# Probabilities by values in a chunk-attention trunk: three float32r products of split operands in place of one float32 product

## The chip, the cores and the metric

One core of one Trainium2 chip runs the whole program in one launch; the other seven cores are idle. The metric is the device time of one execution in microseconds (us). The kernel before was run three times: median 928.1 us, from 927.41 to 928.38.

Two number formats matter. A float32 matmul is carried out by TensorE in two passes, and the profile shows two records for each such instruction. A float32r matmul is one pass over operands that were rounded to fewer mantissa bits when they were written. To get float32 accuracy from float32r, an operand is split: the high part is the value rounded to float32r, the low part is the value minus the high part, again rounded. The product is then high by high plus low by high plus high by low, three passes into the same accumulator.

## The reference

Two layers. Each multiplies the 256 rows of `x` by one wide input projection and cuts the result into the inputs of three groups: chunk attention (8 heads of 128), gated linear attention (GLA, 4 heads), and cross-attention into 256 memory rows (4 heads). Each group output is gated, and one output projection and a LayerNorm follow. Cut to the two groups that the change touches:

```python
def chunk_band_attention(q, k, v, rel_table):
    ...
    scores = jnp.einsum('bnqhd,bnkhd->bnhqk', qc, k_band) * (Dh ** -0.5)
    scores = jnp.where(valid, scores + bias, NEG_INF)
    p = jax.nn.softmax(scores, axis=-1)
    out = jnp.einsum('bnhqk,bnkhd->bnqhd', p, v_band)      # the product that changes

def gla_chunk_recurrence(q, k, v, log_g):                  # reads the GLA values v
    ...
    attn = jnp.einsum('bihd,bjhd,bijhd->bhij', qc, kc, decay)
    o_intra = jnp.einsum('bhij,bjhv->bihv', attn, vc)
    o_inter = jnp.einsum('bihd,bhdv->bihv', qc * jnp.exp(b), state)
    new_state = jnp.exp(b_last)[..., None] * state + jnp.einsum('bjhd,bjhv->bhdv', k_dec, vc)
```

## The kernel before

The program is a stream of weight pieces. Each piece is loaded by SyncE into `raw`, rounded by ScalarE into a high part `wh` (line 116), and VectorE subtracts to get the low part `wl` (line 117, both in `parts`). `raw`, `wh` and `wl` have four buffers each, so at most four pieces stand ready ahead of TensorE. TensorE multiplies each piece by the split activations and accumulates in `acc`, of which there are two. A piece of a 512-wide group is 16 matmuls; a piece of a values group (`w388`, 388 columns) is 12.

TensorE and SyncE run in the order in which the source issues instructions. VectorE and ScalarE run in an order that a scheduler fixed when the program was built. All four work strictly in that order.

The small work of the heads is written as Python generators. After every weight piece the source calls `tick()`, which counts one and lets at most one due generator issue its next step; the number that a generator yields is how many pieces must pass before its next step. At most two generators are active at a time. So head work is slipped in between pieces, and the pieces cover the time that VectorE and ScalarE need between a generator's steps. `finish(gens)` is the other way to drive them: it calls `tick()` until they are done, with no piece in between.

The order in a layer: memory keys and values; queries and keys of GLA (`G_BQK`); `values(0)` and `values(1)`; then the GLA generator is queued; `values(2)`, the queries and keys of heads 0 to 3, and their four `a_head` generators; `values(3)`, and the same for heads 4 to 7; and so on.

`values(i)` computes 388 of the 1552 columns of `asv`: columns 0 to 15 are the low-rank gate input, 16 to 527 the GLA values, 528 to 1551 the values of the eight attention heads. One ScalarE copy (line 792) moves each group from `acc` to `asv`, in float32.

The GLA generator `gla` has this chain, with the yields between its steps in brackets: transpose the gate input (line 339) [2]; gate products, then the cumulative decay `b_` (line 359), the decayed keys `kd` (line 366) and queries `qe` [6]; transpose `kd` (line 392) and copy it (line 394) [2]; `decayed` for the first two of six levels, the state products with the GLA values (line 404), the diagonal products, the states `st` (lines 414 and 417), the diagonal pairs (line 332) [5]; then three rounds, each with the products of two levels, the masked copies of their results (`keep`, line 334) and `decayed` for the next two levels [6]; [3]; and last the products of `pairs` and of `st` with the values and with `qe` (lines 448 and 458). `decayed` is VectorE (line 379), ScalarE twice (lines 381 and 382), VectorE twice (lines 384 and 385), each waiting for the one before.

`a_head` has four steps in one chain: scores and softmax [3], three transposes of the probabilities (line 523) and a ScalarE copy of them into one float32 tile `pT` (line 525) [2], the two float32 products with the values (lines 529 and 530), and a copy out. The first product has 256 moving columns, the second 128, since rows of the first 128 keys serve all 256 queries and those of the second 128 keys serve only the last 128.

Of the kernel before, what the change touches and what calls it, by code (L numbers as in the profile page):

```python
# [8 lines left out]
F32 = mybir.dt.float32  # L9
F32R = mybir.dt.float32r  # L10
# [3 lines left out]
ALU = mybir.AluOpType  # L14
# [4 lines left out]
P = 128  # L19
# [17 lines left out]
def hybrid_trunk_kernel(  # L37
# [7 lines left out]
    pe, dve, act, pool, sp = nc.tensor, nc.vector, nc.scalar, nc.gpsimd, nc.sync  # L45
# [6 lines left out]
    def tick():  # L52

        now[0] += 1
        while True:
            while waiting and len(active) < 2:
                active.append((waiting.pop(0), 0))
            due = [e for e in active if e[1] <= now[0]]
            if not due:
                return  # L60
            active.remove(due[0])
            g = due[0][0]
            after = next(g, None)
# [13 lines left out]
    per = enter("per")  # L77
# [10 lines left out]
    def nm(s):  # L88
        uid[0] += 1
        return f"{s}_{uid[0]}"  # L90

    def mm(o, l, r, start, stop):
        pe.matmul(o, l, r, start=start, stop=stop, skip_group_check=True)  # L93
# [4 lines left out]
    def scratch(shape, dtype=F32):  # L98
        return sc.tile(shape, dtype, name=nm("sc"), tag="sc")
# [14 lines left out]
    def parts(hi, lo, src):  # L114

        act.copy(hi, src)  # L116
        dve.tensor_tensor(lo, src, hi.bitcast(F32), op=ALU.subtract)  # L117
# [189 lines left out]
        pool.dma_start(ng, norm_g[l])  # L307
        return gw, gb, ng

    def gla(gw, gb, ng, gq, gk, lr, asv, yraw):  # L310
        gqf = gq.rearrange("p b t -> p (b t)")
        gkf = gk.rearrange("p b t -> p (b t)")
        pairs = [hd.tile([P, 4, CH], F32, name=nm("pairs"), tag=f"pairs{par}") for par in range(2)]
# [23 lines left out]
        pt = bank()  # L337
# [5 lines left out]
        pl = bank()  # L343
# [45 lines left out]
        pt = bank()  # L389
# [8 lines left out]
        for c in range(3):  # L398
            rs = slice((c % 2) * 64, (c % 2) * 64 + 64)
            t = c // 2  # L400
            for b in range(2):
                for par in range(2):
                    h = 2 * b + par
                    mm(kv[c % 2][par * 64:par * 64 + 64, (t * 2 + b) * P:(t * 2 + b + 1) * P],
                       kdT[rs, t * 2 + b, par * 64:par * 64 + 64],
                       asv[rs, t, 16 + h * P:16 + (h + 1) * P], True, True)
        diagonal = [bank()[:, :256], kv[1][:, 256:]]
        products(gkf, gqf, diagonal)
        st = hd.tile([P, 3, 2, P], F32, name=nm("st"), tag="st")
        for c in range(3):  # L410
            t = c // 2
            src = kv[c % 2].rearrange("p (g c) -> p g c", c=P)[:, t * 2:t * 2 + 2]
# [26 lines left out]
        po = [bank() for _ in range(2)]  # L439
        far = [bank() for _ in range(2)]  # L440
        at = [slice(i * CH, (i + 1) * CH) for i in range(2)]
        for t in range(2):
            for b in range(2):
                g = t * 2 + b
                for half in range(2):
                    for par in range(2):
                        h = 2 * b + par
                        mm(po[half][at[par], g * P:(g + 1) * P], pairs[par][at[half], g],
                           asv[at[half], t, 16 + h * P:16 + (h + 1) * P], g == 0, False)
        for odd, even in ((1, 2), (3, None)):  # L450
            for b in range(2):
                for c in (odd, even):
                    if c is not None:
                        for par in range(2):
                            g = (c // 2) * 2 + b
                            half = c % 2
# [3 lines left out]
        for par in range(2):  # L460
            for half in range(2):
                act.copy(on[par][at[half]], po[half][at[par]].rearrange("p (g c) -> p g c", c=P))
            half = 1 - par
# [33 lines left out]

    SCALE = P ** -0.5

    def a_head(h, load_bias, bias, q, k, asv, y):  # L500

        if h + 2 < 8:
            load_bias(h + 2)
        pb = bank()
        mm(pb[:, 0:128], q[:, 0:128], k[:, 0:128], True, True)
        mm(pb[:, 128:384], q[:, 128:256], k, True, True)
        s = scratch([P, 384])
        dve.scalar_tensor_tensor(s, pb[:, :384], SCALE, bias[h], op0=ALU.mult, op1=ALU.add)  # L508
        mx = small([P, 2], "mx", 4)
        zs = small([P, 2], "zs", 4)  # L510
        own = (slice(0, 128), slice(128, 384))
        for t in range(2):
            dve.tensor_reduce(mx[:, t:t + 1], s[:, own[t]], AX.X, ALU.max, negate=True)  # L513
        for t in range(2):
            act.activation(s[:, own[t]], s[:, own[t]], AF.Exp, bias=mx[:, t:t + 1], accum_out=zs[:, t:t + 1])  # L515
        dve.reciprocal(zs, zs)
        for t in range(2):
            dve.tensor_scalar(s[:, own[t]], s[:, own[t]], zs[:, t:t + 1], None, op0=ALU.mult)
        yield 3

        pt = bank()
        for i in range(3):
            pe.transpose(pt[:, i * P:(i + 1) * P], s[:, i * P:(i + 1) * P], ident)  # L523
        pT = scratch([P, 384])
        act.copy(pT, pt[:, :384])
        yield 2
        po = bank()
        v0 = 528 + h * P
        mm(po[:, 0:256], asv[:, 0, v0:v0 + P], pT[:, 0:256], True, False)
        mm(po[:, 128:256], asv[:, 1, v0:v0 + P], pT[:, 256:384], False, True)  # L530
        act.copy(y, po[:, :256])
        yield 2

# [219 lines left out]
    for l in range(L):  # L753
# [20 lines left out]
        gq = hd.tile([P, 2, T], F32, name=nm("gq"), tag="gq")  # L774
        gk = hd.tile([P, 2, T], F32, name=nm("gk"), tag="gk")
# [4 lines left out]
        gp = gla_inputs(l)  # L780
# [4 lines left out]
            dve.tensor_copy(lmask, lm)  # L785
            dve.tensor_tensor(eye, ident[:, :CH], ident[:, CH:], op=ALU.add)

        asv = per.tile([P, 2, 1552], F32, name=nm("asv"), tag="asv")

        def values(i):  # L790
            acc = as_group(w388[l, i], xq, 388)
            act.copy(asv[:, :, i * 388:(i + 1) * 388], acc[:, :, :388])

        def heads(g):
            t = hd.tile([P, 4, T], F32, name=nm("qk"), tag="qk", bufs=4)
# [5 lines left out]

        lr = hd.tile([P, 2, 48], F32R, name=nm("lr"), tag="qe")
        values(0)
        for i in (0, 32):
            act.copy(lr[:, :, i:i + 16], asv[:, :, :16])
        dve.tensor_tensor(lr[:, :, 16:32], asv[:, :, :16], lr[:, :, :16].bitcast(F32), op=ALU.subtract)
        values(1)
        if l == 0:
            sp.dma_start(res, xn.rearrange("(t p) d -> p t d", p=P))
        bias = {}  # L810
# [7 lines left out]
        if l > 0:  # L818
            finish(gens)
        yraw = [per.tile([P, 4, T], F32, name=nm("yr"), tag=f"yr{i}") for i in range(4)]  # L820
        gens = [[gla(*gp, gq, gk, lr, asv, yraw[0])]]
        waiting.extend(gens[0])
        for half in range(2):
            values(2 + half)
            q = heads(G_AQ0 if half == 0 else G_AQ1)
            k = heads(G_AK0 if half == 0 else G_AK1)
            gens.append([a_head(half * 4 + h, load_bias, bias, q[:, h], k[:, h], asv, yraw[1 + half][:, h]) for h in range(4)])
            waiting.extend(gens[-1])
        q = [hd.tile([P, 4, T], F32R, name=nm("mq"), tag="qk", bufs=4) for _ in range(2)]
        for i, a, b in ws_group(w512[l, G_MQ], xq):  # L830
# [7 lines left out]
        acc = as_group([[w512[l, G_BZ, h * 4 + pc // 2][:, pc % 2 * 512:pc % 2 * 512 + 512] for h in range(2)]  # L838
                        for pc in range(8)], xq, 512)
# [5 lines left out]
        for i, g in ((1, G_AZ0), (2, G_AZ1), (3, G_MZ)):  # L845
            y = operand()
# [150 lines left out]
```

## Time and profile before

| | before |
|---|---|
| median of three runs | 928.1 us |
| the profiled execution, its own time | 928.0 us |
| its span, first to last instruction | 926.2 us |
| TensorE busy | 918.4 us, 99% |
| VectorE busy | 586.0 us, 63% |
| ScalarE busy | 500.4 us, 54% |
| mean granted TensorE clock | 0.998 |

The span is 1.8 us shorter than the time of its execution, which also holds what lies ahead of the first and behind the last instruction. Busy time is a union: overlapping instructions of an engine count once. The ends of matmuls are modelled, and a matmul is still counted busy while the next one streams, so costs on TensorE are best read from start to start. In the rows of the timeline the columns are the start, the time from the first start to the last end of the merged instructions, the engine, the line, the operation, what is written and read, the shape of the stationary and of the moving operand, how many instructions were merged, and in brackets the engine's idle time before and what ended it. A float32 matmul counts as two.

### The profile page before, as it was taken

The numbers are of one execution on the slowest core, as the hardware profiler recorded it, in microseconds if no ns is written. First come the engines' busy times: TensorE is split into PE (matmuls) and PEld (weight loads), VectorE is DVE, ScalarE is ACT, GpSimd is POOL, SyncE is SP. The second block draws the span as 40 slices with busy tenths as digits, with TensorE's granted clock in tenths as the row PEclk, the third lists the DMA queues.
The fourth block names the chain that finished last, engine by engine and source line by source line (L and its number), as shares of the span: only waits on it lengthen the run. The fifth ranks groups of instructions, "written<-read, shape, count | busy, mean of one in ns | idle before, by whom it ended". The sixth has DMA issues, their size and how long they took to land.

```text
span 926.2 us, 14232 instructions
## 1 busy us (share of the span) xinstructions
PE 918.4 (99%) x5500; PEld 806.7 (87%) x5500; DVE 586.0 (63%) x808; ACT 500.4 (54%) x718; POOL 20.4 (2%) x44
## 2 busy tenths in 40 slices
PE   9999999999999999999999999999999999999997
PEld 7889998998888888888888899889888888888885
DVE  6764587656564666555577674966655555766665
ACT  6644485375454675433476445744844555754350
POOL 1000000000000000000000000000000000110000
PEclk9999999999999999999999999999999999999999
DMA  9956865645554566666665466565465545676652
GB/s 310 331 187 174 303 205 161 178 157 197 184 160 160 172 202 203 217 196 192 226 209 203 147 206 193 182 187 183 154 203 171 164 154 160 193 232 215 198 163 92
DMA packets 71253, 178.85 MB, mean 193 GB/s; under 512 B 7304, under 2 KB 31240, under 8 KB 70928
## 3 DMA queue, kind: packets, MB, share of 16 engines
q1 hardware_dynamic: 69120, 173.30, 57.9%
q0 software_dynamic: 1920, 4.36, 1.9%
q8 instruction: 43, 0.70, 0.3%
q10 hardware_dynamic: 144, 0.26, 0.1%
q14 instruction: 26, 0.21, 0.1%
HBM read 175.77 MB, written 2.10 MB: 192 GB/s over the span
## 4 chain that ended last, share of the span: by engine, by line
PE 98%; ACT 0%; DMA 0%; DVE 0%; SPq 0%; issue 0%; ACTq 0%
PE acc L93 89%; PE bk L93 8%; PE bk L523 1%; DMA raw<-w 0%; PE bk L558 0%; PE bk L587 0%; PE bk L491 0%; ACT wh L116 0%; ACT res L636 0%; DVE wl L117 0%; PE bk L392 0%; SPq L177 0%; ACT res L739 0%; PE bk L339 0%; DVE stats L724 0%
## 5 line engine op out<-in xcount | busy, mean ns | idle before, releaser
L117 DVE TENSOR_TENSOR wl<-raw,wh 128x1024 fp32r<-128x1024 f32 (+3 forms) x321 | 370.0, 1155 | 255.3 <-ACT wh L116 250.8
L116 ACT CAST wh<-raw 128x1024 fp32r<-128x1024 f32 (+3 forms) x321 | 318.0, 994 | 332.1 <-PE acc L93 237.5
L93 PE MATMUL acc<-x,wh 128*128 128x512 f32 x1248 | 398.1, 400 | 0.6 <-ACT wh L116 0.6
L93 PE MATMUL acc<-wh,x 128*128 128x512 f32 (+2 forms) x1236 | 357.3, 370 | 0.2
L93 PEld LDWEIGHTS acc<-x,wl 128*128 128x128 f32 x1248 | 234.3, 188 | 55.9 <-DVE wl L117 0.7
L93 PEld LDWEIGHTS acc<-wh,x 128*128 128x128 f32 x1236 | 227.0, 188 | 28.3 <-ACT wh L116 0.7
L93 PE MATMUL acc<-x,wl 128*128 128x256 f32 x1248 | 246.2, 279 | 0.3 <-DVE wl L117 0.3
L93 PE MATMUL acc<-wl,x 128*128 128x512 f32 (+2 forms) x618 | 227.9, 369 | 0.0
L93 PEld LDWEIGHTS acc<-x,wh 128*128 128x128 f32 x1248 | 192.0, 189 | 2.4 <-ACT wh L116 0.8
L93 PEld LDWEIGHTS acc<-wl,x 128*128 128x128 f32 x618 | 116.0, 188 | 14.6 <-DVE wl L117 0.4
L515 ACT ACTIVATE sc<-sc,mx 128x128 f32<-128x128 f32 (+1 forms) x32 | 14.4, 450 | 21.3 <-DVE mx L513 21.3
L508 DVE SCALAR_TENSOR_TENSOR sc<-bk,bias 128x384 f32<-128x384 f32 x16 | 8.9, 556 | 14.6 <-PE bk L93 14.6
L381 ACT ACTIVATE sc<-sc 128x512 f32<-128x512 f32 x12 | 7.6, 633 | 13.2 <-DVE sc L379 13.2
L117 DVE TENSOR_TENSOR x<-sc,x 128x512 fp32r<-128x512 f32 x20 | 13.3, 685 | 0.7 <-ACT x L116 0.7
L620 DVE SCALAR_TENSOR_TENSOR res<-res,acc 128x512 f32<-128x512 f32 x15 | 9.7, 684 | 6.1 <-PE acc L93 6.1
L116 ACT CAST x<-raw 128x1024 fp32r<-128x1024 f32 x5 | 5.3, 1051 | 14.5 <-DMA raw<-memT 12.0
L93 PE MATMUL bk<-qk,qk 128*128 128x128 f32 (+1 forms) x64 | 13.1, 326 | 0.0
L93 PE MATMUL bk<-sc,asv 128*128 128x256 f32 (+1 forms) x64 | 13.0, 326 | 0.0
L262 DVE SCALAR_TENSOR_TENSOR sc<-acc,sc 128x512 f32<-128x512 f32 x19 | 13.0, 682 | 0.0
L117 DVE TENSOR_TENSOR x<-res,x 128x512 fp32r<-128x512 f32 (+2 forms) x14 | 10.5, 765 | 3.6 <-ACT x L116 3.6
L117 DVE TENSOR_TENSOR x<-raw,x 128x1024 fp32r<-128x1024 f32 x5 | 6.1, 1225 | 10.3 <-ACT x L116 10.3
L116 ACT CAST x<-sc 128x512 fp32r<-128x512 f32 x20 | 11.8, 614 | 1.0 <-DVE sc L595 1.0
(205 smaller groups left out, 567.3 us busy)
## 6 DMA issues: line engine op xcount, KB each, us to landing
raw<-w SPq DMA_DIRECT2D x214, 512.0 KB, 4.0
raw<-w SPq DMA_DIRECT2D x64, 388.0 KB, 3.1
raw<-w SPq DMA_DIRECT2D x83, 256.0 KB, 3.3
bias<-relw SPq DMA_DIRECT2D x16, 192.0 KB, 3.6
res<-xT SPq DMA_DIRECT2D x4, 512.0 KB, 5.0
res<-xn SPq DMA_DIRECT2D x1, 2048.0 KB, 8.0
raw<-memT SPq DMA_DIRECT2D x4, 512.0 KB, 4.4
res<-memT SPq DMA_DIRECT2D x6, 256.0 KB, 6.1
```

The lines of the kernel that those rows point to most:

```text
L93: pe.matmul(o, l, r, start=start, stop=stop, skip_group_check=True)
L116: act.copy(hi, src)
L117: dve.tensor_tensor(lo, src, hi.bitcast(F32), op=ALU.subtract)
L262: dve.scalar_tensor_tensor(dst, a, scale, dst, op0=ALU.mult, op1=ALU.add)
L381: act.activation(dd, dd, AF.Abs)
L508: dve.scalar_tensor_tensor(s, pb[:, :384], SCALE, bias[h], op0=ALU.mult, op1=ALU.add)
L515: act.activation(s[:, own[t]], s[:, own[t]], AF.Exp, bias=mx[:, t:t + 1], accum_out=zs[:, t:t + 1])
L523: pe.transpose(pt[:, i * P:(i + 1) * P], s[:, i * P:(i + 1) * P], ident)
L620: dve.scalar_tensor_tensor(r, r, ALPHA, acc, op0=ALU.mult, op1=ALU.add)
```

## The change

The value columns of the eight attention heads are no longer kept in float32. `asv` is split in three: `gv` holds the first 528 columns in float32 (gate input and GLA values); `avh` (named `asv` in rows) holds the high parts of all 1024 attention value columns; `avl` holds the low parts, in two tiles of 512 columns. `values(i)` now makes one float32 copy or one `parts` pair (ScalarE cast, VectorE subtract) for each stretch of columns between the cuts 528 and 1040.

The second `avl` tile has the tag of `gv`: it takes the same memory. So it can be created only behind the last instruction that reads `gv`, which is the last value product of the GLA generator. `values(2)`, which fills columns 776 to 1163, needs that tile. So behind the eight pieces of `values(2)` stands a loop that calls `tick()` until `gla` has passed that point (`done_with`).

In `a_head` the ScalarE copy of the transposed probabilities becomes a `parts` pair, and the two float32 products become six float32r products.

```diff
-    def gla(gw, gb, ng, gq, gk, lr, asv, yraw):
+    def gla(gw, gb, ng, gq, gk, lr, gv, yraw, done_with):
...
                         mm(po[half][at[par], g * P:(g + 1) * P], pairs[par][at[half], g],
-                           asv[at[half], t, 16 + h * P:16 + (h + 1) * P], g == 0, False)
+                           gv[at[half], t, 16 + h * P:16 + (h + 1) * P], g == 0, False)
+        done_with.append(gv)
...
-    def a_head(h, load_bias, bias, q, k, asv, y):
+    def a_head(h, load_bias, bias, q, k, v, y):
...
-        pT = scratch([P, 384])
-        act.copy(pT, pt[:, :384])
+        ph, pl = scratch([P, 384], F32R), scratch([P, 384], F32R)
+        parts(ph, pl, pt[:, :384])
         yield 2
         po = bank()
-        v0 = 528 + h * P
-        mm(po[:, 0:256], asv[:, 0, v0:v0 + P], pT[:, 0:256], True, False)
-        mm(po[:, 128:256], asv[:, 1, v0:v0 + P], pT[:, 256:384], False, True)
+        (vh, vl), last = v, (1, 2)
+        for t, cs, ks in ((0, slice(0, 256), slice(0, 256)), (1, slice(128, 256), slice(256, 384))):
+            for i, (a, b) in enumerate(((vh, ph), (vl, ph), (vh, pl))):
+                mm(po[:, cs], a[:, t], b[:, ks], t == i == 0, (t, i) == last)
...
-        asv = per.tile([P, 2, 1552], F32, name=nm("asv"), tag="asv")
+        gv = per.tile([P, 2, 528], F32, name=nm("gv"), tag="gv")
+        avh = per.tile([P, 2, 1024], F32R, name=nm("asv"), tag="asv")
+        avl = [per.tile([P, 2, 512], F32R, name=nm("avl"), tag="avl")]
+        done_with = []
 
         def values(i):
             acc = as_group(w388[l, i], xq, 388)
-            act.copy(asv[:, :, i * 388:(i + 1) * 388], acc[:, :, :388])
+            if i == 2:
+                while not done_with:
+                    tick()
+                avl.append(per.tile([P, 2, 512], F32R, name=nm("avl"), tag="gv"))
+            c0, c1 = i * 388, (i + 1) * 388
+            cuts = [c0] + [c for c in (528, 1040) if c0 < c < c1] + [c1]
+            for a, b in zip(cuts, cuts[1:]):
+                src = acc[:, :, a - c0:b - c0]
+                if b <= 528:
+                    act.copy(gv[:, :, a:b], src)
+                else:
+                    half, at = divmod(a - 528, 512)
+                    parts(avh[:, :, a - 528:b - 528], avl[half][:, :, at:at + b - a], src)
...
-        gens = [[gla(*gp, gq, gk, lr, asv, yraw[0])]]
+        gens = [[gla(*gp, gq, gk, lr, gv, yraw[0], done_with)]]
...
+            gens.append([a_head(half * 4 + h, load_bias, bias, q[:, h], k[:, h],
+                                [x[:, :, h * P:(h + 1) * P] for x in (avh[:, :, half * 512:], avl[half])],
+                                yraw[1 + half][:, h]) for h in range(4)])
```

The order of TensorE's instructions, first layer, from the transposes of `kd` on. Before, weight pieces (rows that write `acc`) stand between the steps of GLA; `bk` is a bank of small results, `sc` a scratch tile.

```order
L93 MATMUL acc_1211<-x_273,wl_1214 128x256 x2
L392 MATMUL bk_1234<-ident,sc_1109 128x128 x4
L93 MATMUL acc_1211<-x_366,wh_1242 128x512 x2
...
L93 MATMUL bk_1302<-gq_525,gk_526 64x64
L93 MATMUL acc_1211<-x_509,wh_1341 128x512 x2
...
L93 MATMUL acc_1364<-x_509,wl_1433 128x256 x2
L93 MATMUL bk_1453<-sc_1290,sc_1289 64x64
...
L93 MATMUL bk_1454<-sc_1298,sc_1297 64x64
L93 MATMUL acc_1510<-x_273,wh_1512 128x512 x2
```

With the change:

```order
L93 MATMUL acc_1035<-wl_1197,x_509 128x388
L392 MATMUL bk_1213<-ident,sc_1113 128x128 x4
L93 MATMUL bk_1236<-gv_725,sc_1218 64x128 x4
...
L93 MATMUL bk_1237<-gq_525,gk_526 64x64
L93 MATMUL bk_1275<-sc_1225,sc_1224 64x64
...
L93 MATMUL bk_1329<-sc_1318,sc_1317 64x64
...
L93 MATMUL bk_1383<-sc_1380,sc_1379 64x64
...
L93 MATMUL bk_1423<-gv_725,pairs_1054 64x128
...
L93 MATMUL bk_1424<-st_1267,qe_1121 64x128
L93 MATMUL acc_1475<-x_273,wh_1477 128x512 x2
```

All steps of GLA from the transposes of `kd` to the last product of `st` and `qe` now stand in one block behind the last piece of `values(2)`, with no weight piece among them. The second layer has the same block.

VectorE, first layer, from the decayed keys `kd` (line 366) on. Before:

```order
L366 TENSOR_TENSOR sc_1109<-gk_526,sc_1109 128x512
L117 TENSOR_TENSOR wl_1265<-raw_1263,wh_1264 128x1024
L117 TENSOR_TENSOR wl_1342<-raw_1340,wh_1341 128x1024
L379 TENSOR_TENSOR sc_1285<-b_1104 128x512
L117 TENSOR_TENSOR wl_1367<-raw_1365,wh_1366 128x1024
L384 TENSOR_TENSOR sc_1289<-gk_526,sc_1285 128x512
L385 TENSOR_TENSOR sc_1290<-gq_525,sc_1285 128x512
L379 TENSOR_TENSOR sc_1293<-b_1104 128x512
L117 TENSOR_TENSOR wl_1389<-raw_1387,wh_1388 128x1024
L384 TENSOR_TENSOR sc_1297<-gk_526,sc_1293 128x512
```

With the change, the same stretch and, behind the mark, the last level:

```order
L366 TENSOR_TENSOR sc_1113<-gk_526,sc_1113 128x512
L117 TENSOR_TENSOR wl_1533<-raw_1531,wh_1532 128x1024
L379 TENSOR_TENSOR sc_1220<-b_1108 128x512
L117 TENSOR_TENSOR wl_1555<-raw_1553,wh_1554 128x1024
L117 TENSOR_TENSOR avl_727<-acc_1035,asv_726 128x2x264
L384 TENSOR_TENSOR sc_1224<-gk_526,sc_1220 128x512
L385 TENSOR_TENSOR sc_1225<-gq_525,sc_1220 128x512
L379 TENSOR_TENSOR sc_1228<-b_1108 128x512
...
L384 TENSOR_TENSOR sc_1379<-gk_526,sc_1375 128x512
L385 TENSOR_TENSOR sc_1380<-gq_525,sc_1375 128x512
L334 COPY_PREDICATED pairs_1054<-lmask,bk_1383 128x256
```

Behind the fourth weight piece (`wl_1555`) and the first `avl` rows VectorE does nothing but GLA until the last masked copy; its next weight piece stands behind the normalisation of the GLA output. ScalarE has the same gap. In `a_head` one VectorE subtraction of 128x384 is added behind ScalarE's cast of the transposed probabilities, once for each of 16 heads.

More of the change, by code (lines that the diff above doesn't have):

```diff
@@ L405, in gla @@
                        kdT[rs, t * 2 + b, par * 64:par * 64 + 64],
-                       asv[rs, t, 16 + h * P:16 + (h + 1) * P], True, True)
+                       gv[rs, t, 16 + h * P:16 + (h + 1) * P], True, True)
         diagonal = [bank()[:, :256], kv[1][:, 256:]]
@@ L804, in hybrid_trunk_kernel @@
         for i in (0, 32):
-            act.copy(lr[:, :, i:i + 16], asv[:, :, :16])
-        dve.tensor_tensor(lr[:, :, 16:32], asv[:, :, :16], lr[:, :, :16].bitcast(F32), op=ALU.subtract)
+            act.copy(lr[:, :, i:i + 16], gv[:, :, :16])
+        dve.tensor_tensor(lr[:, :, 16:32], gv[:, :, :16], lr[:, :, :16].bitcast(F32), op=ALU.subtract)
         values(1)
@@ L826, in hybrid_trunk_kernel @@
             k = heads(G_AK0 if half == 0 else G_AK1)
-            gens.append([a_head(half * 4 + h, load_bias, bias, q[:, h], k[:, h], asv, yraw[1 + half][:, h]) for h in range(4)])
+            gens.append([a_head(half * 4 + h, load_bias, bias, q[:, h], k[:, h],
+                                [x[:, :, h * P:(h + 1) * P] for x in (avh[:, :, half * 512:], avl[half])],
+                                yraw[1 + half][:, h]) for h in range(4)])
             waiting.extend(gens[-1])
```

## The prediction

> **What bounds the kernel now.** I read the page's busy shares first, then its chain of the work that ended last, then the stretch of the first layer in which GLA runs.
>
> ```profile
> PE 918.4 (99%) x5500; PEld 806.7 (87%) x5500; DVE 586.0 (63%) x808; ACT 500.4 (54%) x718; POOL 20.4 (2%) x44
> PE acc L93 89%; PE bk L93 8%; PE bk L523 1%; DMA raw<-w 0%; PE bk L558 0%; PE bk L587 0%; PE bk L491 0%; ACT wh L116 0%; ACT res L636 0%; DVE wl L117 0%; PE bk L392 0%; SPq L177 0%; ACT res L739 0%; PE bk L339 0%; DVE stats L724 0%
> ```
>
> TensorE is never without work, and the chain is TensorE's own line of matmuls: 89% weight pieces, 8% small products. So a nanosecond added to TensorE's work or to its waiting is a nanosecond of the time, and work on VectorE or ScalarE costs nothing as long as TensorE doesn't come to wait for it. The view by stretches shows the 26 us behind the last piece of `values(2)` in the first layer (start:end, length, then busy time and instructions of TensorE, its weight loads, VectorE, ScalarE and GpSimd; granted clock, share of the DMA engines, GB/s):
>
> ```profile
> 124.33:150.66 26.33, 26.33 (x257) 23.01 (x257) 21.77 (x31) 16.56 (x22) 0.00 (x0) 1.00 0.63 209
> ```
>
> TensorE was busy throughout, VectorE 21.77 us of 26.33. That stretch is where the change bites.
>
> **The change: the block of GLA.** The program's order says that the GLA steps now stand in one block without pieces. Each waits for VectorE, and TensorE, working in order, waits with it. First what GLA costs TensorE by itself, from its timeline before (start, length):
>
> ```profile
> 124.33 0.63 PE L93 MATMUL acc<-x,wh 128*128 128x512 f32 x2
> ...
> 127.13 0.60 PE L392 MATMUL bk<-ident,sc 128*128 128x128 f32 x4
> 127.48 0.71 PE L93 MATMUL acc<-x,wh 128*128 128x512 f32 x2
> ...
> 133.25 0.97 PE L93 MATMUL bk<-asv,sc 64*64 64x128 f32 x21
> ...
> 134.74 0.73 PE L93 MATMUL acc<-x,wh 128*128 128x512 f32 x2
> ...
> 190.86 1.10 PE L93 MATMUL bk<-asv,pairs 64*64 64x128 f32 x32
> ...
> 192.77 0.62 PE L93 MATMUL acc<-wh,x 128*128 128x388 f32 x2
> ```
>
> and from the groups by line and form (count, busy us, mean ns):
>
> ```profile
> L93 PE MATMUL bk<-sc,sc 64*64 64x64 f32 x384 | 7.0, 221 | 0.0
> ```
>
> From start to the next piece's start: transposes 0.35, state and diagonal products 1.49, last products 1.91; the level products are six blocks in the whole program, 7.0 / 6 = 1.17 each, three in a layer. Together 0.35 + 1.49 + 3.5 + 1.91 = 7.2 us a layer, paid before too.
>
> Now the chain that the block waits for, with VectorE's and ScalarE's rows of the same layer before:
>
> ```profile
> 124.69 0.69 DVE L366 TENSOR_TENSOR sc<-gk,sc 128x512 f32<-128x512 f32 x1
> 125.29 2.36 DVE L117 TENSOR_TENSOR wl<-raw,wh 128x1024 fp32r<-128x1024 f32 x2
> ...
> 131.11 0.68 DVE L379 TENSOR_TENSOR sc<-b 128x512 f32<-128x512 f32 x1
> ...
> 133.22 0.69 DVE L384 TENSOR_TENSOR sc<-gk,sc 128x512 f32<-128x512 f32 x1 [0.29 <-ACT sc L382]
> ...
> 134.43 0.68 DVE L379 TENSOR_TENSOR sc<-b 128x512 f32<-128x512 f32 x1
> ...
> 136.17 0.42 DVE L414 COPY st<-bk 128x256 f32<-128x256 f32 x1
> 136.50 0.42 DVE L332 TENSOR_TENSOR pairs<-bk,eye 128x256 f32<-128x256 f32 x1
> ...
> 138.03 0.60 DVE L417 SCALAR_TENSOR_TENSOR st<-st,elast,bk 128x128 f32<-128x128 f32 x2
> 138.55 0.42 DVE L332 TENSOR_TENSOR pairs<-bk,eye 128x256 f32<-128x256 f32 x1
> ...
> 152.77 1.44 DVE L334 COPY_PREDICATED pairs<-lmask,bk 128x256 f32<-128x256 uint8 x4
> ```
>
> ```profile
> 131.89 0.64 ACT L381 ACTIVATE sc<-sc 128x512 f32<-128x512 f32 x1 [0.49 <-DVE sc L379]
> 132.56 0.64 ACT L382 ACTIVATE sc<-sc 128x512 f32<-128x512 f32 x1
> ```
>
> These rows hold the price of one level of `decayed`. VectorE starts line 379 at 131.11, ScalarE follows at 131.89 and 132.56, VectorE's line 384 at 133.22, and the next level's line 379 at 134.43: 3.32 us a level, of which lines 384 and 385 are 1.21 and the wait for ScalarE some 1.5. Before, weight pieces ran on TensorE meanwhile. Let T be the end of `values(2)`, 124.33 in the first layer. Up to there little changes, so line 366 starts at T + 0.36, and by the new order: line 366 takes 0.60, a `wl` 1.18 (2.36 / 2), so the first line 379 starts at T + 2.14. Then 0.60, a `wl` 1.18, the new `avl` subtraction of 528 columns 0.62 (priced like the 512-wide operations), lines 384 and 385 1.21: the second line 379 at T + 5.75. Then 0.60; the state and diagonal operations 0.33 + 0.33 + 0.52 + 0.33 + 0.52 = 2.03; 1.21: the third at T + 9.6. From here four levels at 3.32 remain; the four masked copies (1.44) between some of them fit into the wait for ScalarE. So the last line 385 ends at T + 23.0. Behind it come half a block of products, 0.6 with the hand-over, two masked copies 0.72 and a hand-over of 0.1, and the last products 1.91: the next weight piece starts at T + 26.3. TensorE loses 26.3 - 7.2 = 19.1 us in this layer. The second layer is the same but for its start:
>
> ```profile
> 581.11 0.63 PE L93 MATMUL acc<-x,wh 128*128 128x512 f32 x2
> 582.87 0.69 DVE L366 TENSOR_TENSOR sc<-gk,sc 128x512 f32<-128x512 f32 x1
> ```
>
> Line 366 starts 1.76 behind the end of `values(2)` there, 1.40 later than in the first layer; before, a piece of `wh` and `wl` products covered that. Loss 20.5. **Both layers: +39.6 us.** None of it comes back: TensorE had no other idle time, and the four pieces that stand ready when it resumes are used at the usual rate. They are worth 4 x 4 x 0.70 = 11.2 us (a pair of `wh` and a pair of `wl` products, 265.08 to 265.78 below), enough for ScalarE to copy and square the GLA output and cast the fifth piece, so I price a second wait there at nothing; if that cover fails it costs some 1 us a layer.
>
> **The change: the products.** What one head pays now, and the nearest rows for what it will pay:
>
> ```profile
> 263.96 0.81 PE L93 MATMUL bk<-sc,asv 128*128 128x256 f32 x4
> ...
> 265.08 0.40 PE L93 MATMUL acc<-x,wl 128*128 128x256 f32 x2
> 265.31 0.63 PE L93 MATMUL acc<-x,wh 128*128 128x512 f32 x2
> 265.78 0.39 PE L93 MATMUL acc<-x,wl 128*128 128x256 f32 x2
> 309.64 0.88 PE L93 MATMUL bk<-sc,mv 128*128 128x256 f32 x6
> ...
> 310.83 0.40 PE L93 MATMUL acc<-x,wl 128*128 128x256 f32 x2
> 257.67 0.49 PE L523 MATMUL bk<-ident,sc 128*128 128x128 f32 x3
> ...
> 258.48 0.40 PE L93 MATMUL acc<-x,wl 128*128 128x256 f32 x2
> ```
>
> A pair of `wh` products takes 0.47 (265.31 to 265.78). Taking that off: the four float32 passes of a head cost 265.08 - 263.96 - 0.47 = 0.65, over 768 columns in all, so 0.22 for a pass of 256 and 0.11 for one of 128. Six float32r products of 256 in the memory heads cost 310.83 - 309.64 - 0.47 = 0.72, 0.12 each. No float32r product of 128 columns stands in the trace. Its bounds: 0.06, if time goes with the columns; 0.22, if short ones run at the price of both float32 passes. Three transposes, 128 columns with a fresh 128-column weight load each, cost 258.48 - 257.67 - 0.47 = 0.34, 0.11 each; that is the nearest row, and I take it. A head then costs 3 x 0.12 + 3 x 0.11 = 0.69 against 0.65: **+0.6 us for 16 heads**; at the bounds 0.54 (-1.8 us) and 1.02 (+5.9 us). So even unhindered the products would bring almost nothing.
>
> [...]
>
> The added VectorE work is the `avl` subtractions and 16 subtractions of 128x384, in stretches where VectorE has idle time between its `wl` rows; the probabilities keep their two pieces (5.6 us) of cover. I price it at nothing.
>
> **The change: the clock.** The view by stretches at the end of the program (third from the right: the granted clock), and the first matmuls of the timeline:
>
> ```profile
> 921.00:922.00 1.00, 0.08 (x1) 0.00 (x0) 0.41 (x1) 0.69 (x1) 0.00 (x0) 1.00 0.51 187
> 922.00:923.00 1.00, 0.00 (x0) 0.00 (x0) 0.00 (x0) 0.00 (x0) 0.00 (x0) 0.85 1.02 369
> 923.00:924.00 1.00, 0.00 (x0) 0.00 (x0) 0.00 (x0) 0.00 (x0) 0.00 (x0) 0.50 0.96 309
> ```
>
> ```profile
> 1.05 2.93 PE L93 MATMUL bk<-zeros 128*128 128x128 f32 x12 [1.05 <-DVE eps L752]
> ...
> 4.82 0.40 PE L93 MATMUL acc<-wh,x 128*128 128x256 f32 x2
> ```
>
> The last matmul ends at 921.08, and the granted clock is 0.85 from 922 to 923 and 0.50 behind that: some 1.7 us without matmuls halve it. At the start twelve 128-column passes take 0.24 each, twice their 0.11, and at 4.82 the speed is normal: back to full takes 3 to 3.8 us of work. The block has a hole of about 4.4 us, from the end of the state products near T + 4.0 to the free bank behind the last line 417 at T + 8.4, and holes of 2.8 between the later levels (3.32 less half a block of products). So I expect half clock at its end: half a level block +0.55, and the first 3.4 us of steady work at half speed, +1.7. **+2.3 a layer, +4.6 in both.** Bounds: nothing, and 4.5 a layer if the last products don't count as steady work.
>
> [...]
>
> **Sum.** 928.0 (the profiled execution's own time; the median is 928.1) + 39.6 + 0.6 + 4.6 = 972.8, so 973 us.
>
> **The rivals.** *The clock holds* (25%): the level blocks keep the clock up; no hole in the trace before the last matmul lowered it. 968 us. *Short float32r products are dear* (12%): 0.22 each, 5.3 more than I took: 978 us. *The clock stays low longer, and the resumed pieces wait* (10%): 2.2 and 1 a layer on top: 979 us. *The other side* (3%): VectorE and ScalarE are so far ahead that the block finds its operands ready; `decayed` needs only `b_`, no TensorE result. Then the products decide, at 0.06 a short one: 928.0 - 1.8 = 926 us. It would need line 385 of the sixth level some 23 us earlier than I place it; the order puts it behind line 366, so I give it little.
>
> **How the numbers follow.** My forecast has 50%. Its own error is mostly the hand-overs of the chain, some 2 us a layer. The range 963 to 983 takes in the clock at either bound and the products at either. Of no change (within 0.2%, about 1.9 us, which is what a measurement of this kernel can tell) or faster only the last rival speaks: faster 0.03, same 0.01, slower 0.96.
>
> **What would show it.** Right: TensorE idle some 20 us in each layer, in one stretch from about 124 and from about 602, ended by VectorE lines 384, 385 and 334; VectorE and ScalarE alternating there, with no `wl` or `wh`; a granted clock under 1 in it. The head's six products from start to start near 0.69. Wrong: pieces starting in that stretch, a period of a level far from 3.3 us, or TensorE idle in other stretches, above all behind the 16 added subtractions.

## The result, and the profile after

| | before | with the change |
|---|---|---|
| median | 928.1 us (927.41 to 928.38) | 971.8 us (970.63 to 972.06, 4 runs) |
| ratio, 95% interval | | 1.0468 (1.0455 to 1.0480) |
| span of the profiled execution | 926.2 us | 969.9 us |
| mean granted TensorE clock | 0.998 | 0.972 |

The change makes the kernel 43.7 us slower; 973 us was predicted. The page of the changed kernel, its busy shares, the granted clock in 40 slices and the chain by line:

```profile
PE 931.7 (96%) x5532; PEld 819.1 (84%) x5532; DVE 600.0 (62%) x832; ACT 503.8 (52%) x722; POOL 20.4 (2%) x44
...
PEclk9999978999999999999999999599999999999999
...
PE acc L93 83%; PE bk L93 7%; DVE sc L385 1%; DVE sc L379 1%; DVE pairs L334 1%; DVE sc L384 1%; PE bk L524 1%; DVE wl L117 0%; PE bk L560 0%; PE bk L589 0%; ACT sc L381 0%; ACT sc L382 0%; DMA raw<-w 0%; DVE st L417 0%; ACT wh L116 0%
```

Weight pieces hold 83% of the chain where they held 89%, and the lines of `decayed` and `keep` are new in it. TensorE's share is 96% although its busy time grew: three of the forty slices show a lower clock (7, 8 and 5 tenths), and there its work takes longer (a level's 32 products in the rows below take 1.13 us, and 0.69 in the experiment in which the clock held). The view of waits of TensorE (who waited, for whom; us in total, times, longest) names the place:

```profile
PE bk L93 <- DVE sc L385: 22.5, 12, 2.3
PE bk L392 <- DVE sc L366: 3.3, 2, 2.4
PE bk L93 <- DVE pairs L334: 2.6, 2, 1.3
PE bk L93 <- DVE pairs L332: 1.6, 2, 0.9
PE bk L93 <- ACT sc L394: 1.4, 2, 0.7
```

Twelve waits for line 385 are six levels in two layers; the rest are the other steps of GLA, once a layer. Together they are 31.4 us, 15.7 a layer. The prediction's sign was some 20 us of idle TensorE in each: the block is as long as forecast (below), but at half clock TensorE's own products fill more of it. TensorE's timeline of the first layer, from the last piece of `values(2)` to the first pieces behind the block:

```profile
123.92 0.34 PE L93 MATMUL acc<-wl,x 128*128 128x388 f32 x1
125.20 0.66 PE L392 MATMUL bk<-ident,sc 128*128 128x128 f32 x4 [0.94 <-DVE sc L366]
126.53 0.97 PE L93 MATMUL bk<-gv,sc 64*64 64x128 f32 x21 [0.68 <-ACT sc L394]
...
129.98 0.29 PE L93 MATMUL bk<-sc,sc 64*64 64x64 f32 x2 [1.89 <-DVE sc L385]
131.16 1.12 PE L93 MATMUL bk<-sc,sc 64*64 64x64 f32 x30 [0.88 <-DVE pairs L332]
...
146.79 1.13 PE L93 MATMUL bk<-sc,sc 64*64 64x64 f32 x32 [2.03 <-DVE sc L385]
149.22 2.00 PE L93 MATMUL bk<-gv,pairs 64*64 64x128 f32 x29 [1.30 <-DVE pairs L334]
...
153.07 1.22 PE L93 MATMUL acc<-x,wh 128*128 128x512 f32 x2
...
154.52 0.86 PE L93 MATMUL acc<-x,wh 128*128 128x512 f32 x2
```

T is the end of `values(2)`, read as in the prediction, as the time at which the next piece would have started: its last product starts at 123.92 and takes 0.17 from start to start, so T = 124.09. The next piece starts at T + 29.0. VectorE in the same stretch, two levels in a row and the last:

```profile
136.84 0.68 DVE L379 TENSOR_TENSOR sc<-b 128x512 f32<-128x512 f32 x1
...
140.09 0.68 DVE L379 TENSOR_TENSOR sc<-b 128x512 f32<-128x512 f32 x1
...
143.40 0.68 DVE L379 TENSOR_TENSOR sc<-b 128x512 f32<-128x512 f32 x1
...
146.05 0.68 DVE L385 TENSOR_TENSOR sc<-gq,sc 128x512 f32<-128x512 f32 x1
```

Line 379 returns after 3.25 and 3.31 us. The view by stretches, as in the prediction (start:end, length, busy time of TensorE, its weight loads, VectorE, ScalarE and GpSimd, then the granted clock):

```profile
124.00:130.00 6.00, 2.49 (x63) 1.89 (x61) 6.00 (x9) 3.99 (x7) 0.00 (x0) 1.00 0.75 244
130.00:136.00 6.00, 2.53 (x64) 2.02 (x64) 4.64 (x12) 2.52 (x4) 0.00 (x0) 0.59 0.23 86
136.00:142.00 6.00, 2.26 (x64) 1.92 (x64) 4.76 (x10) 2.36 (x4) 0.00 (x0) 0.50 0.00 0
...
148.00:152.00 4.00, 2.78 (x48) 2.81 (x50) 1.82 (x5) 0.00 (x0) 0.26 (x1) 0.50 0.00 0
...
156.00:160.00 4.00, 4.00 (x25) 3.52 (x24) 0.20 (x2) 3.81 (x15) 0.00 (x0) 1.00 0.00 0
```

The clock is at half from 131.1 us to 155.0, in the pieces behind the block. In the second layer it falls at 605.6, and rises at 632.9. The first wait of that block and two of its stretches:

```profile
604.89 0.66 PE L392 MATMUL bk<-ident,sc 128*128 128x128 f32 x4 [2.36 <-DVE sc L366]
```

```profile
604.00:606.00 2.00, 0.66 (x4) 0.42 (x4) 2.00 (x4) 1.88 (x4) 0.00 (x0) 0.89 0.60 170
606.00:608.00 2.00, 1.78 (x31) 1.78 (x34) 2.00 (x3) 1.43 (x3) 0.00 (x0) 0.50 0.80 264
```

And the six products of one head, with the rows behind them:

```profile
234.86 0.28 PE L93 MATMUL bk<-sc,asv 128*128 128x256 f32 x1
234.98 0.28 PE L93 MATMUL bk<-sc,avl 128*128 128x256 f32 x1
235.10 0.34 PE L93 MATMUL bk<-sc,asv 128*128 128x256 f32 x2
235.28 0.27 PE L93 MATMUL bk<-sc,avl 128*128 128x128 f32 x1
235.39 0.27 PE L93 MATMUL bk<-sc,asv 128*128 128x128 f32 x1
235.50 0.68 PE L93 MATMUL acc<-x,wh 128*128 128x512 f32 x2
236.01 0.40 PE L93 MATMUL acc<-x,wl 128*128 128x256 f32 x2
```

Read as in the prediction: 236.01 - 234.86 - 0.47 = 0.68 us a head, against 0.65 before.

### The profile page after: what moved, and what is told of

Its sections match the earlier page's. It is cut to its first block, busy times and chain, and to the rows that moved or that the text cites. A ratio compares the mean times of both kernels' runs of the same rounds, so it can differ in the third digit from the quotient of the medians.

```text
span 969.9 us, 14328 instructions
## 1 busy us (share of the span) xinstructions
PE 931.7 (96%) x5532; PEld 819.1 (84%) x5532; DVE 600.0 (62%) x832; ACT 503.8 (52%) x722; POOL 20.4 (2%) x44
## 4 chain that ended last, share of the span: by engine, by line
PE 92%; DVE 5%; issue 1%; ACT 1%; DMA 0%; SPq 0%; DVEq 0%; ACTq 0%
PE acc L93 83%; PE bk L93 7%; DVE sc L385 1%; DVE sc L379 1%; DVE pairs L334 1%; DVE sc L384 1%; PE bk L524 1%; DVE wl L117 0%; PE bk L560 0%; PE bk L589 0%; ACT sc L381 0%; ACT sc L382 0%; DMA raw<-w 0%; DVE st L417 0%; ACT wh L116 0%
## 5 line engine op out<-in xcount | busy, mean ns | idle before, releaser
L93 PE MATMUL bk<-sc,sc 64*64 64x64 f32 x384 | 14.3, 317 | 24.1 <-DVE sc L385 22.5
L93 PEld LDWEIGHTS bk<-sc,sc 64*64 64x64 f32 x384 | 11.9, 217 | 26.4 <-DVE sc L385 12.1
L117 DVE TENSOR_TENSOR sc<-bk,sc 128x384 fp32r<-128x384 f32 (+1 forms) x24 | 14.2, 594 | 0.0
```

## The experiments

The theory: the loop in `values(2)` drains GLA in one block, TensorE waits there for the chain of VectorE and ScalarE, and its clock falls meanwhile. The rival: the float32r products, or the VectorE and ScalarE work of splitting, cost the time.

**The loop alone.** The kernel before, with only this added:

```diff
             acc = as_group(w388[l, i], xq, 388)
+            if i == 2:
+                while not done_with:
+                    tick()
             act.copy(asv[:, :, i * 388:(i + 1) * 388], acc[:, :, :388])
```

> The kernel before, with its float32 products and its one value tile of 12 KB, plus only the loop that drains the queue of background work at the end of the third value group until the last linear-attention products are issued. No precision, no product and no split differs from the kernel before. Theory (the loss is the drained block): all of the change's loss but the 0.6 us of the six products, so 970 to 972 us, with the same row of 22 us of PE waiting for line 385's DVE results that the changed kernel has. Rival (the split probabilities, the extra DVE work or the products of float32r cost the time): 928 to 930 us. If both share it, the time lies between.

Measured: 970.27 us (969.09 to 971.05), 1.0460 of before (1.0442 to 1.0477). Its waits:

```profile
PE bk L93 <- DVE sc L385: 20.5, 11, 2.3
PE bk L93 <- DVE pairs L332: 4.7, 2, 3.9
```

Nearly the same block without a single changed product: 42.3 of the 43.7 us. It differs at its start, where the first level waits for line 332, in the first layer for 3.9 us.

**Everything but the block.** All splits and all six products, but the memory of `gv` is reused one group later:

```diff
-        avl = [per.tile([P, 2, 512], F32R, name=nm("avl"), tag="avl")]
+        avl = {528: per.tile([P, 2, 512], F32R, name=nm("avl"), tag="avl"),
+               1040: per.tile([P, 2, P], F32R, name=nm("avl"), tag="avl1")}
...
-            if i == 2:
+            if i == 3:
                 while not done_with:
                     tick()
-                avl.append(per.tile([P, 2, 512], F32R, name=nm("avl"), tag="gv"))
+                avl[1168] = per.tile([P, 2, 384], F32R, name=nm("avl"), tag="gv")
...
-        lrT = sm.tile([48, T], F32R, name=nm("lrT"), tag="lrT")
+        lrT = hd.tile([48, T], F32R, name=nm("lrT"), tag="gb_")
```

> The changed kernel with its six products a head and all its splits, but the low half of the values of heads 4 to 7 no longer waits for the linear-attention values' memory in the third group: head 4's share has a small tile of its own, and only heads 5 to 7 take over that memory, one group and sixteen pieces later, when the linear attention has been issued anyway and the loop finds nothing to drain. Room comes from a small tile that shares another's. Theory (the loss is the drained block): 928.7 us, that is the kernel before plus 16 heads at 0.04 us, with bounds of 926.5 to 933; the PE row of waits for line 385 is gone and the granted clock is back at 1.00 there. Rival (products and splits): 968 us or more, as in the changed kernel.

Measured: 929.81 us (929.06 to 930.14), 1.0018 of before (1.0009 to 1.0027). The waits for line 385 are gone from its view of waits; one is new there:

```profile
PE bk L524 <- DVE sc L519: 0.8, 2, 0.4
```

So splitting and six products, with this edit's smaller tiles, cost 1.9 us against the 0.6 I counted. The products are as in the changed kernel, 0.68 a head, 0.5 us in all. Another 0.8 us is that row: in one head of each layer the transposes of the probabilities (line 524) wait for VectorE's scaling (line 519), which that view before doesn't have. Whether the added VectorE work or only the new order of its instructions makes that wait is not shown. The remaining 0.6 us lies within what these runs can tell.

**Fewer steps left to drain.** Two kernels put more weight pieces between the start of GLA and the loop: `values(2)` behind the queries of heads 0 to 3 (16 pieces, where the change has 8), then behind queries and keys (24).

```diff
         for half in range(2):
-            values(2 + half)
+            if half:
+                values(3)
             q = heads(G_AQ0 if half == 0 else G_AQ1)
+            if half == 0:
+                values(2)
             k = heads(G_AK0 if half == 0 else G_AK1)
```

> The changed kernel with the third value group moved behind the queries of heads 0 to 3, so that sixteen pieces of weights instead of eight stand between the start of the linear attention and the loop. Theory (what is paid is the part of the linear attention's chain that no piece covers): the first two levels are then issued between pieces, four levels and the last products are not; by the changed kernel's trace that is 19.4 us from its second level's products to the next piece, less 2.1 us of a piece and 4.2 us of the block's own PE work, 13 us a layer, so 955 us, 950 to 960. Rival (a fixed price of draining, whatever is left to drain): 970 us as in the changed kernel.

Measured: 950.56 us in one run, near the low end. The part of the block that I misplaced, in TensorE's timeline:

```profile
149.01 1.63 PE L93 MATMUL bk<-sc,sc 64*64 64x64 f32 x96
151.91 0.69 PE L93 MATMUL bk<-sc,sc 64*64 64x64 f32 x32 [1.27 <-DVE sc L385]
155.74 1.22 PE L93 MATMUL bk<-sc,sc 64*64 64x64 f32 x32 [3.14 <-DVE sc L385]
158.90 1.13 PE L93 MATMUL bk<-sc,sc 64*64 64x64 f32 x32 [1.94 <-DVE sc L385]
```

I had expected the first two levels between pieces. All six stand in the block (96 products and three times 32), but the factors of the first three were ready when it began, so three levels are exposed and not four. The price falls with what is left of the chain: a fixed price of draining is out. With `values(2)` one line further down, behind the keys:

> The changed kernel with the third value group moved behind the queries and the keys of heads 0 to 3: 24 pieces of weights between the start of the linear attention and the loop, where the changed kernel has 8 and the kernel with the queries ahead has 16 (which measured 950.6 us). Theory (only what is left of the chain when the loop is reached is paid, and the reuse of the memory is free by itself): left are the last two levels, whose factors are ready by then, four masked copies of 1.43 us on DVE and the last products, so 1.5 to 3 us of idle PE a layer, 932 to 936 us in all, against 929.8 us of the kernel that has the memory of its own. Rival (the price falls with the number of pieces ahead in proportion, 21 us for the first eight): 929 to 930 us. Second rival (the loop costs a fixed sum once it finds anything to drain): 945 us or more.

Measured: 945.07 us (943.78 to 946.12), 1.0185 of before (1.0171 to 1.0199). My number was wrong. Its waits:

```profile
PE bk L524 <- DVE sc L519: 7.9, 2, 4.4
PE bk L93 <- DVE pairs L334: 4.8, 2, 2.4
```

The block's wait is the second row, 2.4 us a layer, as expected; the view by stretches shows the clock untouched around it in the first layer:

```profile
176.00:178.00 2.00, 0.11 (x1) 0.14 (x2) 2.00 (x6) 0.37 (x1) 0.00 (x0) 1.00 0.58 143
178.00:180.00 2.00, 2.00 (x56) 1.78 (x55) 0.49 (x2) 0.28 (x1) 0.47 (x1) 1.00 0.30 121
```

The first row is another place: this edit also brings the heads' first softmax right behind the end of GLA, where ScalarE still squares the GLA output (in the first layer from 182.26 us to 186.3) and loads two tables (1.28 us each, at 186.32 and 187.93), and TensorE waits for it 3.5 and 4.4 us. The time is also the 945 us that the second rival named, a fixed price of draining. To see whether that wait belongs to the reuse of memory or to the heads, the fourth value group was put ahead of them too:

```diff
             if half == 0:
                 values(2)
+                values(3)
```

> The kernel with the queries and keys of heads 0 to 3 ahead, but with the fourth value group too ahead of the heads: heads 0 to 3 are given to the scheduler eight pieces of weights later. The kernel without this change measured 945.1 us, and its trace shows two waits a layer that together make 12.7 us: 2.4 us in the drained block, and 3.5 and 4.4 us some 13 us later, where the first head's transposes wait for DVE's scaled probabilities, because ACT is first held by the linear attention's squares, square root and two table loads. Theory (the second wait is the first head's nearness to the end of the linear attention and not the reuse of the memory): it goes, the first stays, and the time is 934 to 936 us, that is 929.8 us of the kernel with memory of its own plus 4.8. Rival (the wait follows the drained block wherever the heads are): 943 us or more.

Measured: 935.38 us (934.56 to 935.93), 1.0077 of before (1.0060 to 1.0094). Of the two rows its view of waits has the block's alone:

```profile
PE bk L93 <- DVE pairs L334: 4.8, 2, 2.4
```

The second wait was the heads' nearness to the end of GLA, and with it goes the fixed price: this kernel too finds something to drain, and pays 7.2 us in all.

**The clock.** The changed kernel, with extra float32r products of data at hand ahead of each step of the block, so that TensorE isn't idle. `o` is a bank that the next real product overwrites:

```diff
+    def fill(o, n):
+        for x, _, both in filling:
+            for _ in range(n):
+                mm(o[:, :256], x[:, 0, :P], both[:, 0, :256], True, True)
...
             for i in range(2):
+                fill(halves[i][0], 12 if lev + i == 0 else 14)
                 products(*nxt[i], halves[i])
...
+        fill(po[0], 8)
```

This kernel also had 6 ahead of the transposes of `kd` and 4 ahead of the state products:

> The changed kernel with extra work for PE: in the drained block it also multiplies 72 to 120 times 256 columns of an input that is at hand into a bank that the next real product overwrites, about 1.5 us of it ahead of each of the levels' products, so that PE is busy for some 60 to 70% of each level. No result differs. Theory (PE's low clock in the block is a consequence of its idling and costs about 3.4 us a layer: 0.55 us of the last level's products, 1.9 us of the last products and 1.0 us of the first pieces at half the clock): the clock stays near 1.00 and the time falls to about 965 us. First rival (the clock costs nothing, the chain of DVE and ACT sets all): 972 us. Second rival (the clock falls all the same, or falls because of what else runs): the extra products take twice as long, 3.3 us beside 1.1 us of real ones in a level of 3.3 us, PE becomes the bound of the levels and the time rises to about 980 us or more.

Measured: 969.25 us (968.34 to 970.04), 1.0446 of before (1.0430 to 1.0461), clock 0.997, between the expected 965 and the 972 of the first rival. The clock held, at 1.00 in every stretch of the first layer from 120 us to 160; the first level was late, 131.32 where the changed kernel has 129.98. The added lines shift the numbers: line 392 in the rows of the filled kernels is line 385 of the changed one.

```profile
131.32 0.32 PE L93 MATMUL bk<-sc,sc 64*64 64x64 f32 x2 [1.25 <-DVE sc L392]
```

So the two early fills were taken out:

> The filled kernel without the extra products ahead of the transposes and of the state's products: the first extra work comes only ahead of the first level. In the filled kernel the first level began 1.3 us later than in the changed one and the gain of the clock was partly lost by that. Theory (the low clock costs 3.0 us a layer, 1.6 in the last products, 0.9 in the first pieces and 0.5 between the last level and the last products, and the rest of the filled kernel's time is its late first level): the clock stays at 1.00, the first level begins as in the changed kernel, and the time is 965 to 967 us. Rival (the extra work always costs the chain what the clock gives): 969 us, as the filled kernel. The kernel computes the same results.

Measured: 967.30 us (966.80 to 967.67), 1.0425 of before (1.0410 to 1.0439), just above the range. Two levels of the first layer in the view by stretches:

```profile
136.00:142.00 6.00, 4.61 (x91) 4.07 (x90) 5.79 (x13) 2.40 (x4) 0.00 (x0) 1.00 0.01 3
```

and that layer in TensorE's timeline:

```profile
129.85 0.33 PE L93 MATMUL bk<-sc,sc 64*64 64x64 f32 x2 [0.18 <-DVE sc L392]
...
146.83 0.69 PE L93 MATMUL bk<-sc,sc 64*64 64x64 f32 x32 [0.77 <-DVE sc L392]
...
148.73 1.32 PE L93 MATMUL bk<-gv,pairs 64*64 64x128 f32 x29
...
150.96 0.73 PE L93 MATMUL acc<-x,wh 128*128 128x512 f32 x2
...
151.77 0.63 PE L93 MATMUL acc<-x,wh 128*128 128x512 f32 x2
```

The last level's products start where they did (146.83 and 146.79), so the clock costs the levels nothing: VectorE and ScalarE set their period. From there to the next piece it is 4.13 us in place of 6.28, and the first four products of the piece take 0.81 in place of 1.45. By the medians the low clock costs 971.8 - 967.3 = 4.5 us. In the second layer TensorE is slow here too, but only ahead of the first level: the state and diagonal products take 2.32 us from start to the next start (604.16 to 606.48) and the row of 12 extra products behind them 2.38, where the first layer has 1.49 (126.49 to 127.98) and 1.69; from the first level on a row of a level takes 0.69 in both. TensorE's extra 90 products a layer lie in its waits.

**A version without the loop.** Three float32r products only where they meet 256 columns, the float32 product where it meets 128; then only the first half of the values needs low parts, and all fits without sharing. It is the kernel before, with `asv` divided:

```diff
-        mm(po[:, 0:256], asv[:, 0, v0:v0 + P], pT[:, 0:256], True, False)
-        mm(po[:, 128:256], asv[:, 1, v0:v0 + P], pT[:, 256:384], False, True)
+        vh, vl, v1 = v
+        for i, (a, b) in enumerate(((vh, ph), (vl, ph), (vh, pl))):
+            mm(po[:, 0:256], a, b, i == 0, False)
+        mm(po[:, 128:256], v1, pT, False, True)
...
+                    parts(avh[:, cs], avl[:, cs], src[:, 0])
+                    act.copy(av1[:, cs], src[:, 1])
```

> Not the changed kernel's six products: the keys of a head's first 128 rows, which meet 256 queries, as three float32r products of high and low parts (0.35 us by the changed kernel's trace, against 0.43 us for the float32 product of the kernel before), and the keys of the other 128 rows, which meet 128 queries, as one float32 product as before (0.22 us, against 0.28 us for three float32r ones). Only the first half of the values is split, so that all of it fits beside the linear attention's values, and there is no loop. Theory (each product costs on PE what its rows show, and nothing waits): 0.57 us a head against 0.65, 16 heads, 1.3 us less than before, so 926.6 us beside 927.9 of the kernel before. Rival (what the kernel with its own memory lost beyond its products, 1.3 us, comes from the split's extra work on DVE and ACT and comes here too): 927.5 to 929 us. If the float32r products themselves were dear in this place: above 930 us.

Measured: 926.66 us (926.13 to 927.20) beside 927.97, ratio 0.9984 (0.9975 to 0.9993). One head:

```profile
214.55 0.52 PE L93 MATMUL bk<-sc,asv 128*128 128x256 f32 x3
214.90 0.39 PE L93 MATMUL bk<-sc,av 128*128 128x128 f32 x2
215.04 0.71 PE L93 MATMUL acc<-x,wh 128*128 128x512 f32 x2
215.59 0.40 PE L93 MATMUL acc<-x,wl 128*128 128x256 f32 x2
```

215.59 - 214.55 - 0.47 = 0.57 us, as expected, and none of the transposes waits. It is faster than the kernel before by 1.3 us, which is what the rows of the products give.

## Why the prediction was right

**The block.** Predicted 39.6 us. With the clock held the changed kernel takes 39.3 us more than before, of which 0.5 are the products by their rows: 38.8. The steps: a level 3.32 us, measured 3.25 and 3.31; the last line 385 ends at T + 23.0, measured 146.73, T + 22.6; the next piece at T + 26.3 without the clock's share. With that share it is T + 29.0, and the run with the clock held takes 2.1 off it: T + 26.9. The levels were a little quicker than the sum has them, and the tail behind the last of them slower: from the end of line 385 some 4.2 us to the next piece, where I had 3.3. So the block is 0.6 us longer than predicted, and still a little cheaper by the times. The difference is the other side of the subtraction, the 7.2 us that GLA costs TensorE by itself. I took them from the first start of each step to the start of the next piece, without the slower hand-over to and from the pieces that I did count for the heads' products. With it, from one undisturbed pair of products to the next, the kernel before pays 0.43 for the transposes (0.35 in the prediction), 1.67 for the state and diagonal products (1.49), 1.28 for each two levels (1.17) and 2.10 for the last products (1.91): 8.0 us. Then the two blocks with the clock held, 26.9 and 28.2 us, cost 39 us by the rows as by the times. Two terms were off, in opposite directions, so part of the closeness of 39.6 is luck.

**What was wrong in it: the order at the block's start.** I put a hole of 4.4 us between the state products and the first level, since lines 414 to 417 were to come ahead. The first two products of the first level stand already at T + 5.9, and the rest at T + 7.1: its row at 131.16 names line 332, which comes ahead of line 417, as what released it. No wait of TensorE in the block was longer than 2.4 us. The kernel with the loop alone has nearly that hole, 3.9 us; the changed one doesn't.

**The clock.** Predicted 4.6 us, measured 4.5, and the filled kernels show that it is the clock and not the chain. By the rows, from the last level's products to the third pair of `wh` products of the next piece, it is 3.0 us in the first layer (8.67 against 5.64) and 2.2 in the second (7.82 against 5.63). But the 4.4 us hole on which I based it doesn't exist, so the right sum is partly luck. In the first layer the clock fell at 131.1 us behind waits of 0.9, 0.7 and 1.9 us, after 6 us in which TensorE was busy for 2.49 (the row 124 to 130), and stayed at 0.50 while it was busy 2.26 us of 6 at half speed. In the second it fell behind a wait of 2.4 us. In the 3.41 us that end at the fall TensorE was busy for 0.67 and 1.03 us in the two layers of the changed kernel, and for 0.3 in the first layer of the kernel with queries and keys ahead, where the clock fell at 193.2 us in the wait of 3.51; 3.41 us is the step in which the low stretches of these traces come (last section). Whether the busy share is what decides, and where a limit lies, is not shown.

Nor is the 1.7 us that I read at the end of the program a rule. The wait of 2.38 us in the block of the two kernels with queries and keys ahead left the clock at 1.00 in the first layer of both (174 to 180 us in the one, 172 to 184 in the other), while the fall in the second layer of the changed kernel came 0.7 us behind a wait of 2.36.

**The products.** Predicted 0.69 us a head, measured 0.68: the nearest row, the transposes, was the right one to take. Of the three with 128 columns two take 0.11 (235.28, 235.39, 235.50). The first takes 0.06 (235.10 + 0.12 to 235.28), which the piece behind gives back: its second pair starts 0.51 behind the first in place of 0.47. So the bound of 0.06 for all of them is refuted. By the rows the loss is 0.5 us, where the sum has 0.6. That the split costs nothing beside it holds in the changed kernel, which has no wait for line 519 in its view; in the kernel without the block such a wait stands, 0.8 us, whose cause is not shown.

**The cover behind the block.** 11.2 us of ready pieces were to hide the end of GLA. They did: beside the rows shown, the changed kernel's view of waits names only waits at the start and the end of the program. The kernel with queries and keys ahead shows what is late where heads follow too closely: 7.9 us.

**The rivals.** The one in which the clock holds, 968 us, is the filled kernel at 967.3. The one in which the resumed pieces wait, 979 us, is out: no piece behind the block waits in the changed kernel. The rows of 0.11 us refute dear short products, and the twelve waits for line 385 refute operands that are ready when the block begins. The kernels with more pieces ahead are steps towards that last rival: 950.6 us with 16, and 935.4 with 24 and no second wait.

## What to carry to other kernels

Where a tile takes over the memory of another, the price is the latest reader of the old one: read what must be issued before the new tile can exist, and whether anything is left to issue meanwhile. Here sharing 4 KB a partition cost some 42 us, and the arithmetic for which it was shared changed the time by less than 2. Here a float32r product of 128 columns took nearly as long as one of 256 (0.11 against 0.12 us), so splitting a float32 product into three paid only where the moving side was wide: about 0.35 against 0.43 us at 256 columns, but 0.33 (the rest of 0.68) against 0.22 at 128.

## What was not expected of the hardware

The clock halved without a long gap. In the changed kernel it fell behind waits of at most 1.9 us in the first layer and 2.4 in the second, and stayed low for 23.9 and 27.3 us. The low stretches in these traces last a whole number of times 3.41 us: 7 and 8 in the changed kernel, and in the first layer 6 with the loop alone (131.4 to 151.9 us), 4 with queries ahead (153.8 to 167.4) and 1 with queries and keys ahead (193.2 to 196.6). And a wait of 2.38 us kept the clock where one of 2.36 stands just ahead of a fall. So the length of a wait alone doesn't tell; whether it matters where a wait falls between such steps, no run was made to test. Filling the waits with products whose results are thrown away brings the clock of the first layer back to 1.00 (130 to 152 us), and takes 4.5 us off the changed kernel.
